# A two-layer hybrid backbone: gate and up of ten tiles in each of two feed-forwards by a seven-product scheme

## The chip, the cores and the metric

The kernel runs on one core of one Trainium2 chip, in one launch. Its time is the device time of that launch in microseconds (us). Before the change the median of three runs is 1741.17 us (1740.06 to 1743.56).

## The reference, cut to what matters

A sequence of 256 latent and 256 context tokens of width 1024 goes through two layers. Each layer is a half-step SwiGLU feed-forward (hidden width 2816), a token mixer with an output projection, and a second half-step feed-forward. Every one of the three is preceded by an RMS norm whose output is shifted and scaled by values that depend on the conditioning (adaLN), and followed by a gate from the same source. In the last layer only the latent tokens go through the mixer's queries, the output projection and the second feed-forward.

```
def _swiglu(u, w_gate, w_up, w_down):
    return (jax.nn.silu(u @ w_gate) * (u @ w_up)) @ w_down

mod_x = (jax.nn.silu(c) @ w_ada[l] + b_ada[l])[:, None, :]      # nine vectors of 1024: sh, sc, g three times
mod_c = jax.nn.silu(c_ctx) @ w_ada[l] + b_ada[l]                # the same for the context tokens
h  = h  + 0.5 * g1  * _swiglu(_modulate(_rms_norm(h,  norm_ffn1[l]), sh1,  sc1),  w_gate, w_up, w_down)
hc = hc + 0.5 * cg1 * _swiglu(_modulate(_rms_norm(hc, norm_ffn1[l]), csh1, csc1), w_gate, w_up, w_down)
```

## The kernel before, in words

**Data and precision.** Activations lie transposed: 128 partitions by 8 blocks of the width by 512 tokens (columns 0 to 255 latent, 256 to 511 context). Every float32 operand of a large product is kept as a high part that TensorE's fp32r format holds exactly and a low part that is the rest. One 128x128 block of weights against the tokens is then three matmuls in `mm3` (L133 to L136): high by high, high by low, low by high. `U` is the normed and modulated input of a stage, `U[0]` (`Uh`) its high part and `U[1]` (`Ul`) its low part.

**Weights.** `wload` (L126) loads 512 KB over SP's queue into one of three `raw` buffers, copies it on ScalarE to the high half of one of four `split` buffers (L129), and subtracts on VectorE to get the low half (L130). So each 512 KB of weights cost one ScalarE and one VectorE instruction of 128x1024 elements, and three matmuls per 128x128 block wait for them.

**Feed-forward.** `ffn` goes over 22 tiles of 128 hidden units, in parts of 6, 6, 6 and 4. `up_one` computes gate and up of one tile: 24 matmuls into the PSUM tile `pg`, 24 into `pu`. `evac` makes silu(gate) on ScalarE (L371), times up on VectorE (L372), and the high and low halves of `G` (L373, L374). After the first tile of a part the products with the down matrix of the part before it run (`down`, `pd`, L234 adds them to the residual `H`). The last part's down products run in halves of 256 columns together with the next norm. In the second layer's second feed-forward all matmuls have 256 columns. The stages are called here ffn1, mixer and ffn2 of layer 0 and 1.

**adaLN products.** Each of the 72 blocks of 128 modulation values per layer is a row-wise dot product on VectorE: `ada_dve` loads 512 KB over GpSimd's queue into `araw` and runs one scalar_tensor_tensor with accumulation per token (L151, output `ascr`, one instruction for the latent conditioning and one for the context's). `ada_jobs` makes a list of such jobs, and `run_jobs` issues them evenly over the tiles of a feed-forward; ffn1 of layer 0 has 48 blocks, ffn2 of layer 0 32, ffn1 of layer 1 48 (32 of them for the latent conditioning alone), ffn2 of layer 1 none. `cb` holds silu of the conditioning, loaded and computed once per stage.

**Order.** Each engine runs its queue strictly in order. A scheduler places the instructions of the program in the queues; the start of the program and the mixers follow written tables.

Of the kernel before, what the change touches and what calls it, by code (L numbers as in the profile page):

```python
# [18 lines left out]
TOK = SEQ + CTX  # L19
# [4 lines left out]
ABUFS = 8  # L24
# [36 lines left out]
def hybrid_backbone(ctx: ExitStack, tc: tile.TileContext, I, out):  # L61
# [83 lines left out]
    def ada_dve(l, ft, cb, ntok, pool):
        raw = pool.tile([128, 1024], F32, tag="araw", name="araw", bufs=ABUFS)
        with tc.issue_after(marks["pool"]):
            nc.gpsimd.dma_start(raw, I["w_adaT"][l, :, ft * 1024:(ft + 1) * 1024])
        scr = pool.tile([128, 1024], F32, tag="ascr", name="ascr", bufs=1)
        for t in range(ntok):  # L150
            stt(scr, raw, 1.0, cb[:, t, :], op0=ALU.mult, op1=ALU.mult, accum_out=ada[l][:, ft, t:t + 1])  # L151
# [109 lines left out]
    def first_tiles(pool, csel, U, src):  # L261
# [14 lines left out]
        def a(p, i):  # L276

            if i == 0:
                ada_ps[p] = bank("mm", "adaps")
            c, b = divmod(i, 2)  # L280
            raw = pool.tile([128, 4, 256], F32, tag="araw", name="araw", bufs=ABUFS)
# [20 lines left out]
        def w(i):  # L302
            raw = raw_load(src(i), 1024)
            if i < 4:
                t = wp.tile([128, 2, 1024], F32R, tag="split", name="split", bufs=4)
                parts = [(t, 0, 1024)]
            else:
                parts = [(pool.tile([128, 2, 512], F32R, tag="G", name="split0", bufs=10), o, 512) for o in (0, 512)]
            for t, o, n in parts:
                act(t[:, 0, :], raw[:, o:o + n], AF.Copy)  # L310
            sps.append((raw, parts))

        def x(i):
            raw, parts = sps[i]
            for t, o, n in parts:
                tt(t[:, 1, :], raw[:, o:o + n], t[:, 0, :].bitcast(F32), ALU.subtract)
# [19 lines left out]
        def m(i, f):  # L336
            t, o, _ = sps[i][1][f // 4 if i >= 4 else 0]
            wh, wl = (t[:, e, f * 128 - o:f * 128 - o + 128] for e in range(2))
# [11 lines left out]
    def ffn(l, w, halves, pool, U, jobs, after, start=None):  # L350
        both = len(halves) == 2
# [7 lines left out]
        def run_jobs(frac):  # L359
            nonlocal done  # L360
            while done < min(njobs, math.ceil(frac * njobs)):
# [3 lines left out]
        def chunk(src, ft):  # L365
            return wload(src[l, :, ft * 1024:(ft + 1) * 1024])

        def evac(pg, pu):
            g = pool.tile([128, 2, TOK], F32R, tag="G", name="G", bufs=10)
            sil = pool.tile([128, TOK], F32, tag="sil", name="sil", bufs=2)  # L370
            act(sil[:, cols], pg[:, cols], AF.Silu)  # L371
            tt(sil[:, cols], sil[:, cols], pu[:, cols], ALU.mult)  # L372
# [21 lines left out]

        G = {}
        off = [0]

        def down(p0, n, last):
            if not last:
                for d in range(KT):  # L400
                    sp = wload(wd[l, :, off[0]:off[0] + n * 128], n * 128)
                    off[0] += n * 128
                    ps = bank("mm", "pd")
                    for k in range(n):
                        mm3(ps[:, cols], sp[:, 0, k * 128:k * 128 + 128], sp[:, 1, k * 128:k * 128 + 128],
# [3 lines left out]
            else:  # L409
                sps = []  # L410
                for i in range(KT // 2):
                    sps.append(wload(wd[l, :, off[0]:off[0] + n * 256], n * 256))
                    off[0] += n * 256
                def piece(ps, d, h):
                    c = (LAT, CT)[h]
                    o = (d % 2) * n * 128
                    for k in range(n):
                        mm3(ps[:, :256], sps[d // 2][:, 0, o + k * 128:o + k * 128 + 128],
                            sps[d // 2][:, 1, o + k * 128:o + k * 128 + 128],
# [6 lines left out]
        for pi, n in enumerate(PARTS):  # L426
            j = 0
            while j < n:
# [6 lines left out]
                elif ft == 0 and both:  # L435
                    G[0], G[1] = up_two(0)
                    j += 2
                else:
                    G[ft] = up_one(ft)
                    j += 1  # L440
                run_jobs((p0 + j) / (FT - 3))
# [5 lines left out]
            else:  # L447
                run_jobs(1.0)
# [4 lines left out]
    def mixer(l, pool, U):  # L453
# [4 lines left out]
        perm, rope, maskA, maskC, hsel, qkg, sink, nsink, qg8 = (  # L458
            late[n] for n in ("perm", "rope", "maskA", "maskC", "hsel", "qkg", "sink", "nsink", "qg8"))

        def qk_chunk(i):
            return wload(win[l, :, i * 1024:(i + 1) * 1024])

        def rope_lat(x):
            sw = bank("mm", "sw")
            mm(sw[:, :256], perm, x[:, LAT], start=True, stop=True)
            a = pool.tile([128, 256], F32, tag="ra", name="ra", bufs=1)
            b = pool.tile([128, 256], F32, tag="rb_", name="rb_", bufs=1)
# [106 lines left out]
        def v_tok(sps, nk, n, dst, t):  # L575
            ps = bank("mm", "pv")
            for k in range(KT):
                s, o = sps[k // nk], (k % nk) * n
                c = slice(t * 128, t * 128 + 128)
                mm(ps[:, :n], U[0][:, k, c], s[:, 0, o:o + n], start=(k == 0), stop=False)  # L580
                mm(ps[:, :n], U[0][:, k, c], s[:, 1, o:o + n], start=False, stop=False)
                mm(ps[:, :n], U[1][:, k, c], s[:, 0, o:o + n], start=False, stop=(k == KT - 1))
# [188 lines left out]
    def out_proj(l, halves, Y, qcols, after):  # L771
# [5 lines left out]
        for part in range(2):  # L777
            sps = []
            if part == 0:
                for d in range(KT):  # L780
                    if d % 2 == 0:
                        i = d // 2
                        sp = wload(I["w_out"][l, :, i * 1024:(i + 1) * 1024])
# [4 lines left out]
            else:  # L788
                sps = [wload(I["w_out"][l, :, (4 + i) * 1024:(5 + i) * 1024]) for i in range(4)]
# [18 lines left out]
    def ada_jobs(l, mods, pool, ntok=2):  # L808
        jobs = []
        for m in mods:  # L810
            i = MODS.index(m)
            for d in range(KT):
                def job(ft=i * KT + d, m=m, fin=(d == KT - 1)):
                    ada_dve(l, ft, load_cb(pool), ntok, pool)
# [5 lines left out]
    for l in range(DEPTH):  # L820
        last = l == DEPTH - 1
        with tc.tile_pool(name=f"ffn1_{l}", bufs=1) as pool:
            start = None
            if l == 0:
                csel = pool.tile([128, KT, 4, 32], F32, name="csel")
# [18 lines left out]
            else:  # L844
                jobs = ada_jobs(1, ("shm", "scm"), pool) + ada_jobs(1, ("gm", "sh2", "sc2", "g2"), pool, 1)
# [9 lines left out]
        with tc.tile_pool(name=f"ffn2_{l}", bufs=1) as pool:  # L855
            if not last:
                jobs = ada_jobs(0, ("g2",), pool) + ada_jobs(1, ("sh1", "sc1", "g1"), pool)
            else:
                jobs = []
# [22 lines left out]
def _layout(x, c, ctx, c_ctx, w_ada, b_ada, norm_ffn1, w_ffn1_gate, w_ffn1_up, w_ffn1_down, norm_mix, w_in,  # L882
# [13 lines left out]
    for w, (wg, wu, wd) in (("1", (w_ffn1_gate, w_ffn1_up, w_ffn1_down)),  # L896
# [7 lines left out]
        a[f"w_ffn{w}_down"] = np.concatenate(parts, 2)  # L904
    qk = np.concatenate([w_in[:, :, :1024], w_in[:, :, 1024:1152], w_in[:, :, 1280:1408], w_in[:, :, 1536:1920]], 2)
# [43 lines left out]
```

## Time and profile before

| | us |
|---|---|
| median of three runs | 1741.17 |
| the profiled execution's own time | 1742.45 |
| its span in the trace | 1740.5 |
| TensorE busy | 1700.8 |
| VectorE busy | 1180.0 |
| ScalarE busy | 718.5 |
| GpSimd busy | 165.8 |

All durations below come from the one profiled execution. Matmuls overlap in the trace: one of 256 columns is shown with 0.28 us while the next starts 0.12 us later, so the cost of a matmul is the distance from one start to the next, or a window's length over its count. VectorE's instructions overlap a little in the same way. The stages in the trace: ffn1 of layer 0 about 22 to 398 us, the mixer and output projection to 627, ffn2 of layer 0 to 996, ffn1 of layer 1 to 1362, the mixer and output projection to 1529, ffn2 of layer 1 to 1730.

### The profile page before, as it was taken

Reading aid. Unit: us, or ns where it says so; the run is one execution under the profiler, and the core shown is the slowest. Engines: PE = TensorE matmul, PEld = TensorE weight load, DVE = VectorE, ACT = ScalarE, POOL = GpSimd, SP = SyncE. Lnnn points to the kernel's source line nnn. Section 1 sums busy time; section 2 is a strip of 40 time slices with the busy share of each in tenths; the row PEclk is TensorE's granted clock in tenths of the full one; section 3 lists DMA queues with packets and bytes.
Section 4 is the critical chain, followed back from the end, with each engine's and each line's share of the span. In section 5 each row is a group of like instructions: output and inputs, shape, how many; then the busy total and the mean of one; then the engine's idle time right before and its main releaser. Section 6 shows DMA issues by size and latency. Waiting matters only on the chain.

```text
span 1740.5 us, 24756 instructions
## 1 busy us (share of the span) xinstructions
PE 1700.8 (98%) x9572; PEld 1477.5 (85%) x9572; DVE 1180.0 (68%) x2031; ACT 718.5 (41%) x1206; POOL 165.8 (10%) x251
## 2 busy tenths in 40 slices
PE   7999999999999999999999999999999999989997
PEld 4888888889888898888888898888888888889997
DVE  5899963447978869983334599934343787965555
ACT  4322222235888653222222442222222577754443
POOL 0311100012102031100000212100000211100000
PEclk9999999999999999999999999999999999989999
DMA  8877643323223247743333288824332333356663
GB/s 330 309 240 243 197 117 84 110 73 115 58 82 85 75 169 238 236 129 89 108 85 109 63 319 277 321 79 115 85 109 86 99 84 102 109 155 182 182 176 113
DMA packets 76693, 258.37 MB, mean 148 GB/s; under 512 B 8944, under 2 KB 11248, under 8 KB 76192
## 3 DMA queue, kind: packets, MB, share of 16 engines
q1 hardware_dynamic: 54096, 176.72, 33.2%
q0 software_dynamic: 21760, 79.38, 14.3%
q8 instruction: 75, 1.23, 0.3%
q10 hardware_dynamic: 720, 0.69, 0.1%
q14 instruction: 42, 0.34, 0.1%
HBM read 250.47 MB, written 1.05 MB: 145 GB/s over the span
## 4 chain that ended last, share of the span: by engine, by line
PE 89%; DVE 4%; ACT 4%; issue 2%; POOL 1%; DMA 1%; POOLq 0%; DVEq 0%; SPq 0%; ACTq 0%
PE pd L135 8%; PE pd L134 8%; PE pd L136 8%; PE pu L134 8%; PE pu L135 8%; PE pu L136 8%; PE pg L134 8%; PE pg L136 8%; PE pg L135 8%; PE pq L136 1%; PE pq L134 1%; PE pq L135 1%; PE pt L679 1%; DVE split L130 1%; PE pv L580 1%
## 5 line engine op out<-in xcount | busy, mean ns | idle before, releaser
L129 ACT ACTIVATE split<-raw 128x1024 fp32r<-128x1024 f32 (+1 forms) x336 | 332.7, 991 | 546.6 <-PE pu L136 223.2
L130 DVE TENSOR_TENSOR split<-raw,split 128x1024 fp32r<-128x1024 f32 (+1 forms) x336 | 383.9, 1143 | 234.1 <-ACT split L129 233.2
L151 DVE SCALAR_TENSOR_TENSOR ascr<-araw,cb 128x1024 f32<-128x1024 f32 x224 | 273.3, 1220 | 9.9 <-ACT cb L804 7.0
L135 PE MATMUL pd<-G,split 128*128 128x512 f32 (+1 forms) x800 | 272.5, 341 | 0.0
L134 PE MATMUL pd<-G,split 128*128 128x512 f32 (+1 forms) x800 | 271.5, 341 | 0.0
L136 PE MATMUL pd<-G,split 128*128 128x512 f32 (+1 forms) x800 | 271.4, 340 | 0.0
L134 PE MATMUL pg<-Uh,split 128*128 128x512 f32 (+1 forms) x712 | 252.4, 355 | 2.1 <-ACT Uh L225 2.1
L136 PE MATMUL pg<-Uh,split 128*128 128x512 f32 (+1 forms) x712 | 252.3, 354 | 0.0
L135 PE MATMUL pg<-Ul,split 128*128 128x512 f32 (+1 forms) x712 | 252.0, 355 | 0.1
L134 PE MATMUL pu<-Uh,split 128*128 128x512 f32 (+1 forms) x712 | 252.1, 354 | 0.0
L135 PE MATMUL pu<-Ul,split 128*128 128x512 f32 (+1 forms) x712 | 251.9, 354 | 0.0
L136 PE MATMUL pu<-Uh,split 128*128 128x512 f32 (+1 forms) x712 | 251.9, 354 | 0.0
L234 DVE SCALAR_TENSOR_TENSOR H<-pd,ada,H 128x256 f32<-128x256 f32 x272 | 123.3, 479 | 106.9 <-PE pd L136 106.8
L135 PEld LDWEIGHTS pd<-G,split 128*128 128x128 f32 x800 | 151.6, 190 | 17.2
L136 PEld LDWEIGHTS pd<-G,split 128*128 128x128 f32 x800 | 151.4, 190 | 16.9
L134 PEld LDWEIGHTS pd<-G,split 128*128 128x128 f32 x800 | 151.1, 189 | 17.3
L134 PEld LDWEIGHTS pg<-Uh,split 128*128 128x128 f32 x712 | 135.4, 190 | 21.0 <-ACT Uh L225 2.6
L135 PEld LDWEIGHTS pg<-Ul,split 128*128 128x128 f32 x712 | 135.4, 190 | 18.6 <-DVE Ul L226 0.3
L136 PEld LDWEIGHTS pu<-Uh,split 128*128 128x128 f32 x712 | 135.2, 190 | 18.5
L136 PEld LDWEIGHTS pg<-Uh,split 128*128 128x128 f32 x712 | 135.2, 190 | 18.4
L134 PEld LDWEIGHTS pu<-Uh,split 128*128 128x128 f32 x712 | 135.3, 190 | 18.3
L135 PEld LDWEIGHTS pu<-Ul,split 128*128 128x128 f32 x712 | 135.0, 190 | 18.4
(199 smaller groups left out, 2412.6 us busy)
## 6 DMA issues: line engine op xcount, KB each, us to landing
araw<-in_w_adaT POOLq DMA_DIRECT2D x128, 512.0 KB, 5.0
raw<-in_w_ffn_gate SPq DMA_DIRECT2D x88, 512.0 KB, 3.8
raw<-in_w_ffn_up SPq DMA_DIRECT2D x88, 512.0 KB, 3.9
raw<-in_w_ffn_down SPq DMA_DIRECT2D x96, 384.0 KB, 3.2
raw<-in_w_in SPq DMA_DIRECT2D x26, 512.0 KB, 3.5
araw<-in_w_ada SPq DMA_DIRECT2D x16, 512.0 KB, 9.9
raw<-in_w_ffn_down SPq DMA_DIRECT2D x16, 512.0 KB, 3.6
raw<-in_w_out SPq DMA_DIRECT2D x16, 512.0 KB, 3.7
```

Source lines behind the costliest of these rows:

```text
L129: act(sp[:, 0, :n], raw[:, :n], AF.Copy)
L130: tt(sp[:, 1, :n], raw[:, :n], sp[:, 0, :n].bitcast(F32), ALU.subtract)
L134: mm(ps, wh, xh, start=first, stop=False)
L135: mm(ps, wh, xl, start=False, stop=False)
L136: mm(ps, wl, xh, start=False, stop=last)
L151: stt(scr, raw, 1.0, cb[:, t, :], op0=ALU.mult, op1=ALU.mult, accum_out=ada[l][:, ft, t:t + 1])
L234: stt(H[:, d, cols], ps[:, off:off + 256], gate[:, d, half:half + 1], H[:, d, cols], op0=ALU.mult, op1=ALU.add)
L580: mm(ps[:, :n], U[0][:, k, c], s[:, 0, o:o + n], start=(k == 0), stop=False)
L679: nc.tensor.transpose(pt[:, k * 128:(k + 1) * 128], P[t][:, k * 128:(k + 1) * 128], ident)
```

## The change

**Seven products instead of eight.** `FAST` names ffn2 of layer 0 and ffn1 of layer 1, from tile 12 on: ten tiles, taken as five pairs by `up_fast`. For a pair the tokens are cut in two halves (latent, context), the width 1024 in two halves of 512, and the 256 hidden units in two tiles, for gate and up each: a 2x2 by 2x2 block product, computed by seven block products instead of eight (Winograd's form of Strassen's scheme). Each product has 24 matmuls (gate and up, four blocks of 128, three matmuls each) of 256 columns, so a pair has 168 matmuls of 256 columns where it had 96 of 512.

**What the scheme needs besides.** `forms` (after tile 7) and `last_form` (in the first pair) make the sums and differences of `U`: 13 VectorE instructions and 4 ScalarE instructions of 128x1024 elements per feed-forward. Each pair takes four 512 KB blocks of weights (a new copy in DRAM in the order needed, `w_fast`) and makes three more from them with four VectorE subtractions; seven splits instead of four; and the products are put together with eight VectorE instructions of 512 elements and two of 256 (two of these make the low halves of `G`). `w0`, `w1`, `t2` and `cc` have one buffer each.

**Jobs moved.** In these two feed-forwards 65% of the adaLN jobs are issued up to tile 10 and the rest from the second pair on (`run_jobs` in `up_fast`), each product held behind the marked VectorE instruction (`marks["dve"]`). The gate `g2` of layer 1 moves from ffn1 to the first five tiles of ffn2 of layer 1, with its own `cb`. The 224 adaLN products stay 224. `araw` has three buffers in the two feed-forwards instead of eight, `G` eight instead of ten.

**A shifted low half.** The `split` buffer is 2176 elements wide, and wherever the matmuls have 256 columns (the products of the scheme, the last down products, the second half of the output projection, layer 1's queries and output projection, all of ffn2 of layer 1) the low half starts 8 elements, 32 bytes, later than it did.

**Small moves.** The mask `maskC` is loaded in each mixer instead of once, and the rotary temporaries share buffers with the norm's.

```diff
-def wload(src, n=1024):
-    raw = raw_load(src, n)
-    sp = wp.tile([128, 2, 1024], F32R, tag="split", name="split", bufs=4)
-    act(sp[:, 0, :n], raw[:, :n], AF.Copy)
-    tt(sp[:, 1, :n], raw[:, :n], sp[:, 0, :n].bitcast(F32), ALU.subtract)
-    return sp
+def halves_of(pad):
+    t = wp.tile([128, 2176], F32R, tag="split", name="split", bufs=4)
+    o = 1024 + (8 if pad else 0)
+    return t[:, :1024], t[:, o:o + 1024]
+
+def wload(src, n=1024, pad=False):
+    return split(raw_load(src, n), n, pad)
+
+def split(raw, n=1024, pad=False):
+    hi, lo = halves_of(pad)
+    act(hi[:, :n], raw[:, :n], AF.Copy)
+    tt(lo[:, :n], raw[:, :n], hi[:, :n].bitcast(F32), ALU.subtract)
+    return hi, lo
...
+            with tc.issue_after(marks["dve"]) if "dve" in marks else nullcontext():
+                stt(scr, raw, 1.0, cb[:, t, :], op0=ALU.mult, op1=ALU.mult, accum_out=ada[l][:, ft, t:t + 1])
...
+        def run_jobs(ft):
+            nonlocal done
+            if l and not both:
+                frac = ft / 5
+            elif fast == FT:
+                frac = ft / (FT - 3)
+            else:
+                late_ = max(0, ft - fast - 2) / (FT - fast - 4)
+                frac = EARLY * min(1, ft / (fast - 2)) + (1 - EARLY) * late_
...
+        def up_fast(ft):
+            i0 = (ft - fast) * 2
+            src = lambda i: I[f"w_fast{l}{w}"][:, (i0 + i) * 1024:(i0 + i + 1) * 1024]
+            b11, b12 = fm["w"]
+            nc.sync.dma_start(b11, src(0))
+            nc.sync.dma_start(b12, src(1))
+            b22 = raw_load(src(2), 1024)
+            b21 = raw_load(src(3), 1024)
+            t2 = pool.tile([128, 1024], F32, tag="t2", name="t2", bufs=1)
+            A, X, Y, Z = bank("s", "pa"), bank("t", "px"), bank("s", "py"), bank("t", "pz")
...
+            prod(A, b11, "11", True)
+            p1 = c22
+            act(p1, two(A), AF.Copy)
+            tt(b11, b12, b11, ALU.subtract)
+            tt(t2, b22, b11, ALU.subtract)
+            prod(X, t2, "S2", True)
+            marks["dve"] = ins_of(tt(u2, two(X), p1, ALU.add))
+            run_jobs(ft + 0.7)
+            prod(Y, b11, "S1", True)
+            tt(b12, b22, b12, ALU.subtract)
+            prod(Z, b12, "S3", True)
+            u3 = pool.tile([128, TOK], F32, tag="sil", name="u3", bufs=2)
+            tt(two(u3), two(Z), u2, ALU.add)
+            marks["dve"] = ins_of(tt(c22, two(Y), two(u3), ALU.add))
+            run_jobs(ft + 1.4)
+            if ft == fast:
+                last_form()
+            prod(A, b21, "12", False)
...
+            tt(t2, t2, b21, ALU.subtract)
+            X = bank("t", "px2")
+            prod(X, t2, "22", True)
+            tt(u3, u3, X, ALU.subtract)
...
+            prod(Y, b22, "S4", False)
+            tt(u2, two(Y), u2, ALU.add)
...
-                jobs = ada_jobs(1, ("shm", "scm"), pool) + ada_jobs(1, ("gm", "sh2", "sc2", "g2"), pool, 1)
+                jobs = ada_jobs(1, ("shm", "scm"), pool, 2, 3) + ada_jobs(1, ("gm", "sh2", "sc2"), pool, 1, 3)
...
-                jobs = []
+                jobs = ada_jobs(1, ("g2",), pool, 1)
```

**The order of VectorE's queue around tiles 15 and 16 of ffn2 of layer 0, before.** `split` is a low half of weights, `sil` and `G` belong to `evac`; what a row waits for stands in brackets.

```order
L130 TENSOR_TENSOR split_7517<-raw_7515,split_7517 128x1024 [waits DMAHW5_49,PE_49,Activation_49]
L372 TENSOR_TENSOR sil_7427<-sil_7427,pu_7367 128x512 [waits PE_49]
L130 TENSOR_TENSOR split_7546<-raw_7544,split_7546 128x1024 [waits DMAHW6_49,Activation_49]
L374 TENSOR_TENSOR G_7426<-sil_7427,G_7426 128x512 [waits Activation_49]
L130 TENSOR_TENSOR split_7593<-raw_7591,split_7593 128x1024 [waits DMAHW7_49,PE_49,Activation_49]
L372 TENSOR_TENSOR sil_7498<-sil_7498,pu_7438 128x512 [waits PE_49]
L130 TENSOR_TENSOR split_7622<-raw_7620,split_7622 128x1024 [waits DMAHW0_49,Activation_49]
L374 TENSOR_TENSOR G_7497<-sil_7498,G_7497 128x512 [waits Activation_49]
```

For each tile two splits and an evacuation of two instructions stand here, and no adaLN product.

**The same place after: VectorE's queue from the end of the pair 14, 15 to the split for the second product of the pair 16, 17.** `ascr` rows (L163) are adaLN products; `w0` and `t2` are the differences of weights of the next pair, `px`, `py`, `px2` PSUM tiles of products.

```order
L513 TENSOR_TENSOR u3_7530<-u3_7530,px2_7571 128x512 [waits PE_49]
L177 SCALAR_TENSOR_TENSOR amod1_88<-ada1_86,gains_79 128x16 [waits DVE_49]
L492 TENSOR_TENSOR w0_6655<-w1_6656,w0_6655 128x1024 [waits DMAHW5_49]
L515 TENSOR_TENSOR sil_7567<-sil_7567,u3_7530 128x256 [waits Activation_49]
L517 TENSOR_TENSOR cc_7406<-py_7404,cc_7406 128x2x256 [waits PE_49]
L493 TENSOR_TENSOR t2_7649<-raw_7645,w0_6655 128x1024 [waits DMAHW3_49,DVE_49]
L519 TENSOR_TENSOR cc_7406<-cc_7406 128x512 [waits Activation_49]
L524 TENSOR_TENSOR G_7632<-sil_7567,G_7632 128x512
L163 SCALAR_TENSOR_TENSOR ascr_7640,ada1_86<-araw_7638,cb_5954 128x1024 [waits DMASW1_49]
L524 TENSOR_TENSOR G_7635<-cc_7406,G_7635 128x512 [waits Activation_49]
L163 SCALAR_TENSOR_TENSOR ascr_7640,ada1_86<-araw_7638,cb_5954 128x1024 [waits DVE_49]
L140 TENSOR_TENSOR split_7685<-t2_7649,split_7685 128x1024
```

The low half that the second product of the pair 16, 17 needs (`split<-t2`, the last row) now stands behind the whole evacuation of the pair 14, 15 and behind two adaLN products.

**VectorE's queue at the start of ffn2 of layer 1, before.**

```order
L372 TENSOR_TENSOR sil_13269<-sil_13269,pu_13209 128x256 [waits DMASW3_49,DMASW4_49,DMASW2_49,DMASW5_49,DMASW1_49,DMASW6_49,DMASW0_49,DMASW7_49,PE_49,Activation_49]
L130 TENSOR_TENSOR split_13344<-raw_13342,split_13344 128x1024 [waits DMAHW2_49,Activation_49]
L374 TENSOR_TENSOR G_13268<-sil_13269,G_13268 128x256 [waits Activation_49]
L130 TENSOR_TENSOR split_13373<-raw_13371,split_13373 128x1024 [waits DMAHW3_49,Activation_49]
L372 TENSOR_TENSOR sil_13335<-sil_13335,pu_13275 128x256 [waits PE_49]
L130 TENSOR_TENSOR split_13410<-raw_13408,split_13410 128x1024 [waits DMAHW4_49,Activation_49]
L374 TENSOR_TENSOR G_13334<-sil_13335,G_13334 128x256 [waits Activation_49]
L130 TENSOR_TENSOR split_13439<-raw_13437,split_13439 128x1024 [waits DMAHW5_49,Activation_49]
```

The first split of the third tile stands right behind the first tile's `sil`.

**The same place after.**

```order
L394 TENSOR_TENSOR sil_14233<-sil_14233,pu_14173 128x256 [waits DMASW3_49,DMASW4_49,DMASW2_49,DMASW5_49,DMASW1_49,DMASW6_49,DMASW0_49,DMASW7_49,PE_49,Activation_49]
L163 SCALAR_TENSOR_TENSOR ascr_14243,ada1_86<-araw_14241,cb_14238 128x1024 [waits DMASW4_49]
L396 TENSOR_TENSOR G_14232<-sil_14233,G_14232 128x256 [waits Activation_49]
L163 SCALAR_TENSOR_TENSOR ascr_14247,ada1_86<-araw_14245,cb_14238 128x1024 [waits DMASW5_49,DVE_49]
L394 TENSOR_TENSOR sil_14310<-sil_14310,pu_14250 128x256 [waits PE_49]
L163 SCALAR_TENSOR_TENSOR ascr_14317,ada1_86<-araw_14315,cb_14238 128x1024 [waits DMASW6_49,DVE_49]
L396 TENSOR_TENSOR G_14309<-sil_14310,G_14309 128x256 [waits Activation_49]
L163 SCALAR_TENSOR_TENSOR ascr_14321,ada1_86<-araw_14319,cb_14238 128x1024 [waits DMASW7_49,DVE_49]
L140 TENSOR_TENSOR split_14327<-raw_14325,split_14327 128x1024 [waits DMAHW2_49]
L140 TENSOR_TENSOR split_14356<-raw_14354,split_14356 128x1024 [waits DMAHW3_49]
L140 TENSOR_TENSOR split_14397<-raw_14395,split_14397 128x1024 [waits DMAHW4_49]
```

Four adaLN products (L163) and the second tile's `sil` and `G` now stand ahead of that split.

## Rows read from the trace of the kernel before

**Rows 1.** The page: busy time by engine, TensorE's granted clock in 40 slices, the chain by engine
```profile
PE 1700.8 (98%) x9572; PEld 1477.5 (85%) x9572; DVE 1180.0 (68%) x2031; ACT 718.5 (41%) x1206; POOL 165.8 (10%) x251
...
PEclk9999999999999999999999999999999999989999
...
PE 89%; DVE 4%; ACT 4%; issue 2%; POOL 1%; DMA 1%; POOLq 0%; DVEq 0%; SPq 0%; ACTq 0%
```

**Rows 2.** Windows: busy us (count) of PE, PEld, DVE, ACT, POOL, clock, DMA, GB/s, DMA share, GB/s
```profile
200.00:300.00 100.00, 100.00 (x442) 82.80 (x442) 59.15 (x90) 26.29 (x33) 1.07 (x2) 1.00 0.39 113
839.50:904.00 64.50, 64.50 (x286) 53.43 (x285) 21.22 (x24) 17.59 (x23) 0.00 (x0) 1.00 0.32 90
1600.00:1700.00 100.00, 100.00 (x836) 100.00 (x835) 58.23 (x78) 44.83 (x63) 0.00 (x0) 1.00 0.63 183
1526.00:1543.00 17.00, 12.37 (x71) 11.73 (x70) 12.73 (x25) 7.80 (x17) 2.86 (x3) 0.70 0.41 124
```

**Rows 3.** Groups of VectorE by line and shape: count | busy us, mean ns | idle before
```profile
L130 DVE TENSOR_TENSOR split<-raw,split 128x1024 fp32r<-128x1024 f32 x232 | 284.7, 1227 | 171.6 <-ACT split L129 171.5
L151 DVE SCALAR_TENSOR_TENSOR ascr<-araw,cb 128x1024 f32<-128x1024 f32 x224 | 273.3, 1220 | 9.9 <-ACT cb L804 7.0
L372 DVE TENSOR_TENSOR sil<-sil,pu 128x256 f32<-128x256 f32 x22 | 9.3, 421 | 11.6 <-PE pu L136 11.6
```

**Rows 4.** Timeline of VectorE in ffn1 of layer 0: start, duration, instruction, [idle before]
```profile
102.08 1.22 DVE L151 SCALAR_TENSOR_TENSOR ascr<-araw,cb 128x1024 f32<-128x1024 f32 x1
103.23 0.69 DVE L374 TENSOR_TENSOR G<-sil,G 128x512 fp32r<-128x512 f32 x1
103.83 1.22 DVE L151 SCALAR_TENSOR_TENSOR ascr<-araw,cb 128x1024 f32<-128x1024 f32 x1
104.97 0.95 DVE L130 TENSOR_TENSOR split<-raw,split 128x768 fp32r<-128x768 f32 x1
```

**Rows 5.** Timeline of VectorE around one feed-forward tile, ffn2 of layer 0
```profile
883.21 0.69 DVE L372 TENSOR_TENSOR sil<-sil,pu 128x512 f32<-128x512 f32 x1 [2.58 <-PE pu L136]
884.31 1.23 DVE L130 TENSOR_TENSOR split<-raw,split 128x1024 fp32r<-128x1024 f32 x1 [0.40 <-ACT split L129]
885.45 0.68 DVE L374 TENSOR_TENSOR G<-sil,G 128x512 fp32r<-128x512 f32 x1
```

**Rows 6.** Timeline of VectorE, the first tiles of ffn2 of layer 1
```profile
1547.06 0.42 DVE L372 TENSOR_TENSOR sil<-sil,pu 128x256 f32<-128x256 f32 x1 [3.97 <-PE pu L136]
1547.89 1.23 DVE L130 TENSOR_TENSOR split<-raw,split 128x1024 fp32r<-128x1024 f32 x1 [0.41 <-ACT split L129]
1549.03 0.42 DVE L374 TENSOR_TENSOR G<-sil,G 128x256 fp32r<-128x256 f32 x1
1549.69 1.23 DVE L130 TENSOR_TENSOR split<-raw,split 128x1024 fp32r<-128x1024 f32 x1 [0.24 <-ACT split L129]
1551.09 0.42 DVE L372 TENSOR_TENSOR sil<-sil,pu 128x256 f32<-128x256 f32 x1 [0.17 <-PE pu L136]
1551.42 1.22 DVE L130 TENSOR_TENSOR split<-raw,split 128x1024 fp32r<-128x1024 f32 x1
```

**Rows 7.** Timeline of TensorE between the output projection and ffn2, layer 1
```profile
1531.46 0.35 PE L201 MATMUL ss<-ones,acc 128*128 128x2 f32 x2 [2.22 <-DVE acc L193]
1536.67 0.58 PE L134 MATMUL pg<-Uh,split 128*128 128x256 f32 x1 [1.11 <-ACT Uh L225]
1537.05 0.41 PE L134 MATMUL pu<-Uh,split 128*128 128x256 f32 x1
1537.26 0.41 PE L134 MATMUL pg<-Uh,split 128*128 128x256 f32 x1
```

**Rows 8.** Timeline of VectorE, the last tile of ffn2 of layer 0
```profile
970.25 0.69 DVE L372 TENSOR_TENSOR sil<-sil,pu 128x512 f32<-128x512 f32 x1 [2.58 <-PE pu L136]
972.49 0.68 DVE L374 TENSOR_TENSOR G<-sil,G 128x512 fp32r<-128x512 f32 x1
```

**Rows 9.** The page: DMA issues by group, KB each, median us to landing
```profile
araw<-in_w_adaT POOLq DMA_DIRECT2D x128, 512.0 KB, 5.0
```

More of the change, by code (lines that the diff above doesn't have):

```diff
@@ L1 @@
 import math
-from contextlib import ExitStack
+from contextlib import ExitStack, nullcontext
 import numpy as np
@@ L350, in ffn @@
     def ffn(l, w, halves, pool, U, jobs, after, start=None):
+        fast = FAST.get((l, w), FT)
+        gbufs = 8 if fast < FT else 10
         both = len(halves) == 2
@@ L393, in up_two, with forms, whole, parts @@
             return [evac(pss[0], pss[1]), evac(pss[2], pss[3])]
+        fm = {}
+        def forms():
+            LO, HI = slice(0, 4), slice(4, 8)
+            rows = lambda t: t.rearrange("p (a b) -> p a b", a=4)
+            block = [pool.tile([128, 1024], F32R, name=f"S{i}", bufs=1) for i in range(6)]
+            w1, w2 = fm["w"] = [pool.tile([128, 1024], F32, name=f"w{i}", bufs=1) for i in range(2)]
+            w3 = pool.tile([128, 1024], F32, tag="t2", name="w3", bufs=1)
+            def whole(t, k, c):
+                with tc.issue_after(marks["dve"]):
+                    tt(rows(t), U[0][:, k, c].bitcast(F32), U[1][:, k, c].bitcast(F32), ALU.add)
+            def parts(n, i, t):
+                h, lo = block[2 * i:2 * i + 2]
+                act(h, t, AF.Copy)
+                tt(lo, t, h.bitcast(F32), ALU.subtract)
+                fm[n] = (rows(h), rows(lo))
+            whole(w1, LO, CT)
+            whole(w2, HI, CT)
+            tt(w2, w1, w2, ALU.add)
+            parts("S1", 0, w2)
+            whole(w3, LO, LAT)
+            tt(w1, w3, w1, ALU.subtract)
+            parts("S3", 1, w1)
+            tt(w3, w2, w3, ALU.subtract)
+            parts("S2", 2, w3)
+            for n, k, c in (("11", LO, LAT), ("12", HI, LAT), ("22", HI, CT)):
+                fm[n] = (U[0][:, k, c], U[1][:, k, c])
@@ new lines, in last_form @@
+        def last_form():
+            h, lo = fm["S4"] = U[0][:, 0:4, CT], U[1][:, 0:4, CT]
+            rows = lambda t: t.rearrange("p (a b) -> p a b", a=4)
+            a, b = (rows(pool.tile([128, 1024], F32, tag="araw", name="s4", bufs=3)) for _ in range(2))
+            tt(a, U[0][:, 4:8, LAT].bitcast(F32), U[1][:, 4:8, LAT].bitcast(F32), ALU.add)
+            tt(b, fm["S2"][0].bitcast(F32), fm["S2"][1].bitcast(F32), ALU.add)
+            tt(a, a, b, ALU.subtract)
+            act(h, a, AF.Copy)
+            tt(lo, a, h.bitcast(F32), ALU.subtract)
@@ L400, in down @@
                 for d in range(KT):
-                    sp = wload(wd[l, :, off[0]:off[0] + n * 128], n * 128)
+                    sp = wload(wd[l, :, off[0]:off[0] + n * 128], n * 128, not both)
                     off[0] += n * 128
@@ L440, in ffn @@
                     j += 1
-                run_jobs((p0 + j) / (FT - 3))
+                run_jobs(p0 + j)
+                if fast < FT and p0 + j == fast - LEAD:
+                    forms()
                 if pend is not None:
@@ L457, in mixer @@
         win = I["w_in"]
-        perm, rope, maskA, maskC, hsel, qkg, sink, nsink, qg8 = (
-            late[n] for n in ("perm", "rope", "maskA", "maskC", "hsel", "qkg", "sink", "nsink", "qg8"))
+        perm, rope, maskA, hsel, qkg, sink, nsink, qg8 = (
+            late[n] for n in ("perm", "rope", "maskA", "hsel", "qkg", "sink", "nsink", "qg8"))
+        maskC = pool.tile([128, 2, 256], F32, name="maskC", bufs=1)
+        nc.gpsimd.dma_start(maskC, I["maskC"])
         def qk_chunk(i):
-            return wload(win[l, :, i * 1024:(i + 1) * 1024])
+            return wload(win[l, :, i * 1024:(i + 1) * 1024], pad=i < 8 and not ctxq)
         def rope_lat(x):
@@ L788, in out_proj @@
             else:
-                sps = [wload(I["w_out"][l, :, (4 + i) * 1024:(5 + i) * 1024]) for i in range(4)]
+                sps = [wload(I["w_out"][l, :, (4 + i) * 1024:(5 + i) * 1024], pad=True) for i in range(4)]
                 def piece(ps, d, h):
```

105 lines of the change are left out of this document (69 added, 36 removed).

## The prediction

> **What bounds the kernel now.** I read the page's busy times and its chain first: TensorE is busy for 98% of the span, it makes 89% of the chain that ended last, and no other engine has more than 4% of it [rows 1]. Then the windows, one per kind of stage, because an average over the span hides what each stage lacks: in a dense stretch of 512 columns TensorE never rests while VectorE has 59.15 us of work in 100; in the tiles 13 to 18 of ffn2 of layer 0, just where the change goes, VectorE works only 21.22 us of 64.5 [rows 2]. So time is TensorE's matmuls, and what is taken from them is time as long as VectorE, which makes every low half, stays ahead. The timelines then give the price of one instruction and the slack that a tile leaves.
>
> **Prices.** A matmul of 512 columns: 100 us / 442 = 0.2262 us; the middle window gives 64.5 / 286 = 0.2255, and a few records can be missing, so 0.2266. One of 256 columns: 100 / 836 = 0.1196, taken as 0.120 [rows 2]. So half the columns cost 53%, not half. On VectorE I take the distance from start to start: 1.14 us for 1024 elements (1547.89 to 1549.03) and 0.33 for 256 (1551.09 to 1551.42) [rows 6], 0.60 for 512 and 1.145 for an adaLN product (102.08 to 103.23 to 103.83 to 104.97) [rows 4]; the means of 1.227 and 1.220 us [rows 3] overlap the next instruction.
>
> **Gain on TensorE.** Per feed-forward ten tiles x 48 = 480 matmuls x 0.2266 = 108.8 us become five pairs x 168 = 840 x 0.120 = 100.8: 8.0 us less, 16.0 for both. One eighth fewer products gives only 7% because of the dearer columns. By column count alone the gain would be 13.6 each.
>
> **Load on VectorE.** A pair has eleven instructions of 1024 (seven splits, four differences), eight of 512 and two of 256: 12.54 + 4.80 + 0.66 = 18.0 us, against 168 x 0.120 = 20.2 us of TensorE. Before, two tiles took four splits and four of 512, 4.56 + 2.40 = 7.0 us, beside 21.8. So 11% of room is left in a pair, and into it the change puts adaLN products: by the order of VectorE's queue 22 in the pairs 14, 16 and 18 of ffn2 of layer 0, 25.2 us, and 14 in those of ffn1 of layer 1. Between these three pairs no down products stand, so TensorE needs 60.5 us and VectorE 54.0 + 25.2 = 79.2 in the first.
>
> How much of this comes through as waiting I take from the order, in us from the first product of pair 14. VectorE's combination of the second product can start at 2 x 2.88 = 5.76. From there to the low half for pair 18's second product stand 18 of 1024, 16 of 512, 4 of 256, 16 adaLN products: 20.5 + 9.6 + 1.3 + 18.3 = 49.7, with 0.2 of small ones 49.9. So that half is ready at 55.7. TensorE would ask for it at 2 x 20.16 + 2.88 = 43.2. After it come six products, 17.3, less 0.7 that may be issued ahead (the high-half matmuls): the stretch ends at 72.3 to 72.7 instead of 60.5, 12.2 lost. In ffn1 of layer 1 the same stretch has 18 of 1024, 15 of 512, 4 of 256 and 9 adaLN products: 41.3, ready at 47 to 48, end 64.2: 3.7 lost. Here the evacuation rows of before matter: sil and G stood at 883.21 and 885.45 with 2.58 us of idle time ahead [rows 5], and nothing waited; in the new order the evacuation and two adaLN products stand ahead of the split that the next product needs.
>
> **What is hidden.** The forms of U, 13 x 1.14 = 14.8 us of VectorE in each feed-forward, lie under tiles 8 to 11 (43.5 us of TensorE) and pair 12; the tightest split there has about 0.6 us to spare, so I take 0, and up to +2 if that goes. The products that leave these late tiles for early ones go to stretches with 40 idle us in 100 [rows 2]: 0. ScalarE gets seven copies in place of four, under 20.2 us: 0. SP issues the four blocks of a pair; the loads of w0 and w1 wait for their single buffers but are issued a product or more ahead of use: 0. GpSimd's loads take 5.0 us to land [rows 9]; three buffers in place of eight hold the loads back for as long as VectorE is late, and a group of four products needs about what three buffers hold: 0, up to +2. The mask and rotary buffers: 0, up to +1 in each mixer.
>
> **Tails.** The last pair ends with two evacuations in place of one: its last low half of G comes 24.6 us after the pair's start, 4.4 after its last product, where before G started 2.24 us after sil [rows 8]. The last down products are cut in pieces that need G in turn; I take 0.9 us per feed-forward, 1.8 in all, 0 to 4.
>
> **Start of ffn2 of layer 1.** In before the split of the third tile starts at 1547.89, in the shade of the second tile's matmuls, and the second tile's sil at 1551.09 [rows 6]. In the new queue that sil and four adaLN products stand ahead of the split: after 1551.09, 0.33 + 1.145 + 0.33 + 1.145 and a ScalarE hand-over put it near 1555.2. TensorE wants it at 1551.1, or 0.7 later as above: +3.4. The cb of this stage lands under the norm; if it came late, up to +3 more.
>
> **Clock.** Where TensorE rested 2.22 us, then worked on small matmuls between waits, the granted clock fell: the window has 0.70 [rows 2], and matmuls of 256 columns then stand 0.213 apart (1537.05 to 1537.26) [rows 7]: the level of 1.2 GHz. The stall of ffn2 of layer 0 falls into lumps, one of about 4 us at the start of pair 16, others of 3 to 5 us later. One stretch at the lower level that costs 1.7 us is my value, since rows show such a stretch only after idle time beside sparse work; 0 to 12 are the bounds. The Trainium skill has the rule (page "TensorE: Matmul & The Clock Gate", section "HAM oscillation — how this bites in real kernels") that idle gaps between bursts throttle TensorE again; rows 7 agree for the norm, no row shows it inside a feed-forward. By it every lump would cost, which is a rival below.
>
> **The shifted low half.** No row of before has such a layout, so it is bounded. 0.213 at half the clock is 256 columns at 1.2 GHz with no gap; at full clock that would be 0.1067, and the measured 0.120 has 0.0133 of something on top. Outside the pairs 2736 matmuls of 256 columns get the shift (by the code's loops 1584 in ffn2 of layer 1, 576 last down products of the other stages, 384 of the output projections, 192 queries). If it took all of the gap: -36 us; if only from the third of them that loads the low half: -12; and in the two pairs per feed-forward that TensorE bounds, 672 matmuls, -9 or -3 more. It could cost as well: up to +10. I take 0, since the one pitch of 0.120 stands in ffn2 of layer 1 with weights, and equally where activations are the weights. The Trainium skill (page "TensorE: Matmul & The Clock Gate", section "Step-by-step: what each phase is for") says that TensorE reads weights and moving data by two independent ports, so a load takes nothing from the running matmul; by that rule the shift is worth 0; the trace can't tell.
>
> **Sum.** -16.0 + 12.2 + 3.7 + 1.8 + 3.4 + 1.7 = +6.8 on the profiled execution's 1742.45, so 1749.3. That execution is 1.3 above the median of the runs, so 1748 for a median.
>
> **Rivals.**
> 1. The shift makes 256 columns cheaper. For it: 0.0133 us of every matmul is not streaming, and it is gone at half the clock. Against it: no row varies with the layout. With a third of it, 1748 - 12 - 3 = 1733; with all, 1748 - 36 - 9 = 1703. It decides the sign from about 0.002 us per matmul on (7 us / 3408): below that it is still slower. This is the case on the other side.
> 2. VectorE keeps up: the products and splits of one pair slide under the next, or the real distances are shorter in a dense queue. For it: the stretch before has two thirds of VectorE free. Against it: 79.2 us do not go into 60.5. Without the 15.9 of stalls and the clock's 1.7, 1748 - 17.6 = 1730. It needs VectorE's distances at about three quarters of the rows.
> 3. The stalls throttle TensorE. Four or five lumps in the first feed-forward and one or two in the second, each followed by a stretch at 1.2 GHz that costs 1.7 to 3 us, less what VectorE catches up meanwhile: 1748 + 8 to 14, about 1758. For it the window at 0.70; against it that a slow TensorE gives VectorE the time it lacked.
>
> **How the numbers follow.** Forecast 0.42 (own range 1741 to 1755), rival 1 0.30, rival 2 0.17, rival 3 0.11. What this measurement can tell is 0.2%, 3.5 us: under 1737.7 faster, over 1744.7 slower. The forecast gives 0.31 slower, 0.10 the same, 0.01 faster; rival 1 0.26 faster, 0.03 the same, 0.01 slower; rival 2 0.16 faster, 0.01 the same; rival 3 0.11 slower. Together faster 0.43, same 0.14, slower 0.43. The range 1716 to 1757 leaves out the large gain of rival 1, about 0.08, and the far half of rival 3 with the unlikely sums of bounds, about 0.09.
>
> **What would show it.** The windows of pairs 14 to 18: TensorE idle with the releaser VectorE `split`, about 12 us in ffn2 of layer 0 and 4 in ffn1 of layer 1, VectorE at 95% or more there. Dense stretches of ffn2 of layer 1 with 0.120 per matmul, else rival 1. An idle row of 3 us at about the third tile of ffn2 of layer 1. The granted clock at 1.00 in pairs 14 to 18 but for one dip, else rival 3. The prediction is wrong if the dense 256-column distance changes, or if TensorE's idle time in the pairs is under 5 us.

## The result: 0.8% slower, and the profile after

The changed kernel takes 1755.57 us (median, 1753.34 to 1757.34) against 1741.81 of before: a ratio of 1.0078, 95% interval 1.0061 to 1.0096. The profiled execution took 1754.82 us. The page of the changed kernel, next to [rows 1]:

```profile
PE 1690.9 (96%) x10292; PEld 1500.0 (86%) x10292; DVE 1319.8 (75%) x2187; ACT 767.0 (44%) x1265; POOL 167.1 (10%) x253
...
PE 78%; DVE 11%; ACT 5%; issue 4%; DMA 2%; POOL 1%; POOLq 0%; DVEq 0%; SPq 0%; ACTq 0%
```

TensorE is busy 9.9 us less, and yet the end comes 12.5 us later: VectorE has 11% of the chain where it had 4%. Where it waits is seen in windows of the changed kernel, the pairs 14, 16 and 18 of ffn2 of layer 0 and a stretch of ffn2 of layer 1 (columns as in [rows 2]).

```profile
849.73:869.61 19.88, 19.88 (x169) 19.87 (x168) 17.32 (x27) 6.59 (x8) 1.59 (x3) 1.00 0.57 169
869.61:896.12 26.51, 22.86 (x170) 22.12 (x169) 24.90 (x36) 10.68 (x14) 1.58 (x3) 0.87 0.43 132
896.12:926.49 30.37, 24.67 (x170) 23.97 (x169) 28.73 (x38) 11.84 (x16) 1.05 (x2) 0.83 0.45 132
1600.00:1700.00 100.00, 100.00 (x848) 100.00 (x847) 59.41 (x79) 45.07 (x63) 0.00 (x0) 1.00 0.64 186
```

A pair without waiting takes 19.88 us; these three took 76.76 in place of 59.64: 17.1 us lost. VectorE is at 94 and 95% in the second and third. TensorE is idle for 3.65 + 5.70 us by its busy time, and the granted clock is 0.87 and 0.83, so part of each window runs at 1.2 GHz. The same three pairs of ffn1 of layer 1, where fewer products stand, and what follows them:

```profile
1225.50:1245.38 19.88, 19.88 (x169) 19.88 (x168) 16.87 (x24) 6.78 (x9) 2.11 (x4) 1.00 0.71 210
1245.38:1268.07 22.69, 21.63 (x170) 20.31 (x169) 22.56 (x30) 9.60 (x13) 2.11 (x4) 1.00 0.57 183
1268.07:1293.32 25.25, 23.41 (x175) 22.40 (x173) 22.88 (x33) 10.98 (x15) 1.59 (x3) 0.93 0.43 136
1293.32:1325.06 31.74, 31.74 (x142) 26.29 (x141) 23.28 (x35) 9.35 (x11) 0.00 (x0) 1.00 0.37 112
```

The third window also holds four of the 144 matmuls of the down products: the other 140 take the 31.74 us of the fourth, and all 144 take 32.67 us without waiting (a window of e5_downs below), so 0.93 us. Without these, 66.89 us in place of 59.64: 7.2 lost. The waits by name, TensorE's timeline in the changed kernel (the idle time before a row and its releaser stand in brackets):

```profile
877.38 0.58 PE L147 MATMUL px<-S,split 128*128 128x256 f32 x1 [2.01 <-DVE split L140]
...
899.29 0.58 PE L147 MATMUL pa<-Uh,split 128*128 128x256 f32 x1 [2.77 <-DVE split L140]
...
906.27 0.58 PE L145 MATMUL px<-S,split 128*128 128x256 f32 x1 [2.78 <-ACT split L139]
...
1564.77 0.58 PE L147 MATMUL pg<-Uh,split 128*128 128x256 f32 x1 [3.30 <-DVE split L140]
```

The third is named after ScalarE, which copies a high half that VectorE had first to make as a difference. The fourth stands at the third tile of ffn2 of layer 1. VectorE's timeline ahead of the first of them:

```profile
871.99 0.70 DVE L519 TENSOR_TENSOR cc<-cc 128x512 f32<-128x512 f32 x1
872.60 0.70 DVE L524 TENSOR_TENSOR G<-sil,G 128x512 fp32r<-128x512 f32 x1
873.20 1.23 DVE L163 SCALAR_TENSOR_TENSOR ascr<-araw,cb 128x1024 f32<-128x1024 f32 x1
...
874.94 1.23 DVE L163 SCALAR_TENSOR_TENSOR ascr<-araw,cb 128x1024 f32<-128x1024 f32 x1
...
876.09 1.24 DVE L140 TENSOR_TENSOR split<-t,split 128x1024 fp32r<-128x1024 f32 x1
```

No idle time stands between these rows: the split that TensorE asks for comes last, in the order that the change shows.

### The profile page after: what moved, and what is told of

Its sections match the earlier page's. It is cut to its first block, busy times and chain, and to the rows that moved or that the text cites. A ratio compares the mean times of both kernels' runs of the same rounds, so it can differ in the third digit from the quotient of the medians.

```text
span 1753.0 us, 26434 instructions
## 1 busy us (share of the span) xinstructions
PE 1690.9 (96%) x10292; PEld 1500.0 (86%) x10292; DVE 1319.8 (75%) x2187; ACT 767.0 (44%) x1265; POOL 167.1 (10%) x253
## 4 chain that ended last, share of the span: by engine, by line
PE 78%; DVE 11%; ACT 5%; issue 4%; DMA 2%; POOL 1%; POOLq 0%; DVEq 0%; SPq 0%; ACTq 0%
PE pd L147 8%; PE pd L146 8%; PE pd L145 8%; PE pg L147 5%; PE pg L145 5%; PE pu L147 5%; PE pu L145 5%; PE pg L146 5%; PE pu L146 5%; DVE ascr L163 3%; DVE split L140 3%; PE pq L147 1%; PE pq L145 1%; PE pq L146 1%; PE pt L820 1%
## 5 line engine op out<-in xcount | busy, mean ns | idle before, releaser
L140 DVE TENSOR_TENSOR split<-raw,split 128x1024 fp32r<-128x1024 f32 (+1 forms) x316 | 358.8, 1138 | 138.5 <-ACT split L139 137.3
L163 DVE SCALAR_TENSOR_TENSOR ascr<-araw,cb 128x1024 f32<-128x1024 f32 x224 | 273.6, 1221 | 2.3 <-DMA araw<-in_w_adaT 0.8
L147 PE MATMUL pg<-Uh,split 128*128 128x512 f32 (+1 forms) x552 | 190.5, 345 | 3.3 <-DVE split L140 3.3
L145 PE MATMUL pg<-Uh,split 128*128 128x512 f32 (+1 forms) x552 | 190.5, 346 | 2.5 <-ACT Uh L237 2.1
L146 PE MATMUL pg<-Ul,split 128*128 128x512 f32 (+1 forms) x552 | 189.5, 344 | 0.1
L145 PE MATMUL pu<-Uh,split 128*128 128x512 f32 (+1 forms) x552 | 189.5, 343 | 0.0
L147 PE MATMUL pu<-Uh,split 128*128 128x512 f32 (+1 forms) x552 | 189.4, 343 | 0.0
L146 PE MATMUL pu<-Ul,split 128*128 128x512 f32 (+1 forms) x552 | 189.0, 342 | 0.0
L159 POOL DMA_DIRECT2D araw<-in_w_adaT x128 | 68.0, 532 | 706.7 <-DVE ascr L163 653.6
L147 PEld LDWEIGHTS pg<-Uh,split 128*128 128x128 f32 x552 | 105.1, 190 | 15.7 <-DVE split L140 3.5
L145 PEld LDWEIGHTS pg<-Uh,split 128*128 128x128 f32 x552 | 105.2, 191 | 15.4 <-ACT Uh L237 2.6
L146 PEld LDWEIGHTS pg<-Ul,split 128*128 128x128 f32 x552 | 105.2, 191 | 12.3 <-DVE Ul L238 0.3
L145 PEld LDWEIGHTS pu<-Uh,split 128*128 128x128 f32 x552 | 104.4, 189 | 12.2
L146 PEld LDWEIGHTS pu<-Ul,split 128*128 128x128 f32 x552 | 104.4, 189 | 12.1
```

The costliest lines, as they stand in the source:

```text
L140: tt(lo[:, :n], raw[:, :n], hi[:, :n].bitcast(F32), ALU.subtract)
L145: mm(ps, wh, xh, start=first, stop=False, skip_group_check=go_on)
L146: mm(ps, wh, xl, start=False, stop=False, skip_group_check=go_on)
L147: mm(ps, wl, xh, start=False, stop=last, skip_group_check=go_on)
```

## The experiments

**Where the products stand: all early.** One number changed:

```diff
-LEAD, EARLY = 4, 0.65
+LEAD, EARLY = 4, 1.0
```

> All adaLN jobs of the two feed-forwards are issued up to tile 10, none in the pairs 14 to 20; everything else as changed. Theory (adaLN products fill VectorE's queue in the pairs 14 to 18, TensorE waits 11.9 us and runs 5.0 us of lower clock in ffn2 of layer 0, about 4 to 5 together in ffn1 of layer 1): the three pairs take 59.6 to 61 us instead of 76.8 and 64.3, so 1755.6 - 16 - 4 = 1735 to 1738, granted clock 1.00 in the pairs. Rival A (the single buffers w0, w1, t2 and cc chain one pair to the next, whatever VectorE else does): the idle rows in the pairs stay, 1752 to 1756. Rival B (the products only move the wait: tiles 0 to 11 now stall on VectorE): pairs free, but as much idle time in tiles 8 to 12, 1748 or more.

Measured 1754.26 us (ratio to before 1.0070, 1.0058 to 1.0082): hardly better, and yet the three pairs take 19.88 us each. The time went to the early tiles, rival B. A window of this run in ffn2 of layer 0, where the forms of U are made:

```profile
760.00:780.00 20.00, 15.55 (x70) 12.56 (x68) 20.00 (x28) 6.68 (x8) 1.59 (x3) 0.95 0.40 131
```

VectorE is full there, and TensorE's next row comes after 4.45 us of waiting for a split. In ffn1 of layer 1 idle rows of 4.18 and 2.07 us stand ahead of the pairs, where the changed kernel has none. The products had only met another crowded stretch; this run alone could not tell overload from a rule that products cost anywhere.

**The same products in the down stretches.**

```diff
-            run_jobs(ft + 0.7)
...
-            run_jobs(ft + 1.4)
...
+                    if fast < FT and p0 >= 6:      # in down, after each d
+                        run_jobs(FT, ((p0 // 6 - 1) * KT + d + 1) / (2 * KT))
```

> The late 35% of the adaLN jobs are issued in the down products of the second and third part (one step after each of 16 groups) instead of in the pairs; the early 65% stay. By the order 12 and 10 products of ffn2 of layer 0 and 7 and 7 of ffn1 of layer 1 stand there, none between the pairs 14 and 18. Theory (a stretch stalls when VectorE's work in that stretch exceeds TensorE's; with all jobs early it was the tiles up to 9 that overflowed): the downs have 32.4 us of TensorE and 13.3 of VectorE each, so they take the products free, the pairs take 59.6 to 61 us, and 16.9 + 5 us go: 1755.6 - 22, 1732 to 1737. Rival A (the pairs wait on their single buffers and their chain): idle rows stay in the pairs, 1750 or more. Rival B (any place for the products costs the same, since a held-back product always meets a split): idle rows in the downs, 1748 or more.

Measured 1730.68 us (0.9932, 0.9920 to 0.9945): 24.9 us less than the change. The theory had 22; the 17.1 and 7.2 us lost in the pairs are 24.3. Windows of this run, the three pairs and the down products behind them:

```profile
850.09:869.97 19.88, 19.88 (x169) 19.88 (x168) 16.45 (x19) 8.49 (x10) 0.00 (x0) 1.00 0.36 106
869.97:889.85 19.88, 19.88 (x170) 19.88 (x169) 18.48 (x22) 10.39 (x13) 0.00 (x0) 1.00 0.34 100
889.85:909.73 19.88, 19.88 (x170) 19.88 (x169) 15.83 (x20) 10.18 (x14) 0.00 (x0) 1.00 0.47 134
909.73:942.40 32.67, 32.67 (x147) 27.04 (x145) 32.17 (x52) 8.89 (x11) 1.05 (x2) 1.00 0.39 117
```

The scheme, its buffers and its chain are the same; without adaLN products in these pairs TensorE never waits and the clock stays. The down stretch takes them to 32.17 us of 32.67, without a loss. So the scheme is worth its gain, and the change lost it by the place of 36 instructions.

**g2 two tiles later.** `frac = max(0, ft - 2) / 5` in place of `ft / 5`.

> The eight g2 jobs of ffn2 of layer 1 are issued from tile 3 to tile 7 instead of 1 to 5. Theory (four products and two evacuation steps ahead of the third tile's split cost 3.3 us of idle time and 1.1 us of lower clock): no idle row over 1 us at the third tile, 1755.6 - 4.4 = 1751. Rival (the stage waits for its cb, its loads or ScalarE, wherever the products stand): an idle row of 3 us stays, perhaps later, 1755.

Measured 1748.72 us (1.0047, 1.0033 to 1.0061): 6.9 less, more than the 4.4 expected; the idle row of 3.30 us is gone, and none over 1.1 stands in its place. In the profiled executions ffn2 of layer 1 takes 194.9 us in place of 200.6, 5.7 less. One of the six runs took 1755.03 us, so the size beyond 4.4 lies within what the two medians leave open.

**The shift.** In e2_noshift `o = 1024` for all; e7_shiftonly is the kernel before with the shift alone (but for the rotary temporaries' buffers and the wider `split` tile, which stay as changed in all runs on the kernel before); e8_shiftall has `o = 1024 + 8` for every split; e9_shift64 has 16 elements in place of 8.

> The changed kernel with every low half of weights at its old place, 4096 bytes behind the high half; the order of all queues is the same. Theory (the shift is worth 0.0018 us of every matmul of 256 columns, 0.1182 against 0.1200): in 1600 to 1700 us 836 matmuls again instead of 848; 2736 x 0.0018 = 4.9 us outside the pairs and 1 to 3 in them, so 1761 to 1763. Rival (the denser count comes from something else in this kernel, or is given back as waiting for VectorE): 1755.6 and 846 to 848 matmuls in the window.

> The kernel before, with the low halves shifted by 32 bytes wherever the matmuls have 256 columns, and nothing else; the order of every queue is that of before. Theory (0.0018 us of each of 2736 matmuls): 1742.3 - 4.9, 1736 to 1739, 846 to 848 matmuls in 1600 to 1700 us. Rival (the shift pays only in the changed kernel's queues): 1742.

> As e7_shiftonly, but every low half is shifted, those for 512 columns too. Theory I (the shift helps each load of a low half, whatever streams meanwhile): 512 columns fall from 0.2266 by 0.0018, so about 10 us less than e7_shiftonly, 1727. Theory II (it helps only where a weight load and 256 columns take about the same time): 442 matmuls in 200 to 300 us as before, the time of e7_shiftonly within 2 us.

> As e7_shiftonly, with a shift of 64 bytes in place of 32. Theory I (any shift off the 4096 bytes between high and low half does it): 846 to 848 matmuls in 1600 to 1700 us and the time of e7_shiftonly, 1739.6 within 2. Theory II (the 32 bytes matter, the place within a 64-byte line): 836 matmuls and the time of before, 1742.7 within 2.

Without it the change takes 1759.24 us (1.0099 of before, 1.0086 to 1.0112), 3.7 more, less than was expected, and the window from 1600 to 1700 us has 835 matmuls where it had 848. In ffn2 of layer 0 the two kernels take the same time from norm to norm (377.0 and 377.1 us): there, what the shift gives in the pairs goes into waiting. With the shift alone the kernel before takes 1739.63 (0.9983, 0.9974 to 0.9992), with 64 bytes 1739.09 (0.9980, 0.9971 to 0.9989). Shifted everywhere it takes 1768.74 (1.0149, 1.0136 to 1.0163): neither theory had a loss. Windows of ffn2 of layer 1 with 32 bytes (e7_shiftonly):

```profile
1600.00:1700.00 100.00, 100.00 (x847) 100.00 (x846) 59.94 (x80) 44.62 (x63) 0.00 (x0) 1.00 0.65 188
```

with 64 bytes (e9_shift64):

```profile
1600.00:1700.00 100.00, 100.00 (x852) 100.00 (x851) 59.55 (x79) 45.71 (x64) 0.00 (x0) 1.00 0.64 187
```

and 512 columns with a shift of 32 bytes (e8_shiftall), in ffn1 of layer 0:

```profile
200.00:300.00 100.00, 100.00 (x430) 80.39 (x429) 60.59 (x93) 25.66 (x32) 1.61 (x3) 1.00 0.39 112
```

Against 836 and 442 [rows 2]: 256 columns gain 1.3 or 1.9%, 512 columns lose 2.8%.

**Everything but the scheme.** `FAST = {}`.

> The seven-product scheme is not used anywhere; everything else of the change stays: shifted low halves, products held behind the marked instruction, three araw buffers, g2 in ffn2 of layer 1. Theory (outside the pairs the change is -4.9 us of shift, +4.4 at the third tile of ffn2 of layer 1, about +1 elsewhere): 1741.8 + 0.5, so 1741 to 1743. Rival (the job order, the three buffers or the held-back products cost by themselves): 1747 or more.

Measured 1749.09 us (1.0038, 1.0026 to 1.0050): the rival. With `FAST` empty the jobs are also spread over the tiles as before and `G` has ten buffers again, so this run doesn't test the 65% order. e5_downs, with the scheme, takes 18.4 us less than this run. Of the 6.8 us over before, -3.1 are the shift and +6.9 g2 by the runs above, so 3.0 were to be found, or 4.2 with the 5.7 of the profiled executions. Two runs on the kernel before looked for them: the mask loaded in each mixer (e10_mask), and the products held behind the marked instruction (e11_hold).

> The kernel before, with the mask of the neighbourhood heads loaded on GpSimd's queue at the start of each mixer instead of once. Theory (GpSimd's two additions of the mask start 0.7 to 2.2 us later and then run beside VectorE's low halves of U, whose two instructions take 2.95 us in place of 0.87 to 1.91): about 1.0 us in each mixer, 1742.7 + 2.0 = 1744 to 1746. Rival (the longer VectorE instructions have slack behind them): 1742 to 1743.5.

> The kernel before, with each adaLN product held back behind the marked evacuation instruction in VectorE's queue, nothing else. Theory (holding back bunches the products of the first feed-forward between down products: an idle row of 0.9 to 1.2 us at about 126 us, and little elsewhere): 1743.5 to 1745. Rival (the idle row there comes from the buffers): 1742 to 1743.

The mask: 1744.57 us (1.0014, 1.0005 to 1.0023), +1.9 as expected. TensorE's wait for the next split of weights grows from 0.53 to 1.77 us in the first mixer and from 0.26 to 1.56 in the second. VectorE and GpSimd at the start of the first mixer of e10_mask:

```profile
402.62 2.97 DVE L238 SCALAR_TENSOR_TENSOR Ul<-t,ada,Uh 128x256 fp32r<-128x256 f32 x2
...
402.57 2.73 POOL L742 TENSOR_TENSOR bias<-bias,maskC 128x512 f32<-128x512 f32 x2 [2.69 <-DMA bias<-in_rpb]
```

Holding back: 1742.38 us (0.9998, 0.9990 to 1.0007), nothing; that theory falls. The idle row of 0.90 us at 126 us in the changed kernel, which neither e10_mask nor e11_hold has, and 1 to 2 us with it, stay unexplained; the three `araw` buffers were not run by themselves.

**The parts together.** e6_all is e5_downs with g2 later, the mask on SP's queue and the products held back only where the scheme is; e12_best has the 64-byte shift besides.

> As e5_downs, with the g2 jobs of ffn2 of layer 1 from tile 3 on, the mask loaded over SP's queue and the products held back only in the two feed-forwards with the scheme. Theory: the single gains add up: 1734 - 6.9 of g2 - about 1 of the first feed-forward - 0 to 2 of the mixers: 1724 to 1728, and faster than before. Rival (the gains share one cause, such as the clock's level, and do not add): 1730 to 1735.

> e6_all with the 64-byte shift of e9_shift64. Theory (852 matmuls in 100 us of ffn2 of layer 1 instead of 847 with 32 bytes, 0.0007 us of each of 4416 matmuls of 256 columns): 1723.1 - 3, 1719 to 1722. Rival (no difference between the two shifts, as the times of e7_shiftonly and e9_shift64 lie within each other's spread): 1722 to 1724.

Measured 1723.07 us (0.9894, 0.9879 to 0.9909) and 1721.26 (0.9887, 0.9870 to 0.9903): both faster than before and after. The gains add: the 7.6 us from e5_downs to e6_all are close to g2's 5.7 to 6.9 and the mask's 1.9. The second shift's 1.8 us are not separated from the spread of the two runs.

## Why the prediction was right

The sign and its cause were right: VectorE could not do its pairs and the products in TensorE's time. The size was not: the profiled executions differ by +12.4 us, predicted +6.8. The prediction gave slower and faster the same chance, 0.43, and the measured 1755.57 lies above the forecast's own range (1741 to 1755) and near the end of the whole one (1757). That the sign and the range held is in part luck. By its steps:

| step | predicted | measured |
|---|---|---|
| matmuls of the ten pairs | -16.0 | -18.8: ten times 19.88 against two tiles, 96 x 0.2266 = 21.76; about 3 of it the shift |
| waiting and clock, ffn2 of layer 0 | +12.2 +1.7 | +17.1 |
| waiting, ffn1 of layer 1 | +3.7 | +7.2 with its clock |
| tails | +1.8 | +1.9: idle rows of 0.73, 0.11 and 0.11 in each feed-forward |
| third tile of ffn2 of layer 1 | +3.4 | 3.30 idle in the trace; +5.7 to +6.9 by e3_g2later |
| mask in the mixers | 0 | +1.9 |
| shift outside the pairs | 0 | -3.1 |

The measured steps add up to +11.9 to +13.1. Most of what the sum missed is in the clock, in ffn1 of layer 1 and behind the third tile; the shift and the cheaper pairs took some of it back.

The first mis-sized term is the clock: "one stretch at the lower level that costs 1.7 us". The stretches of the changed kernel in which the granted clock is 0.50, three in ffn2 of layer 0 and one in ffn1 of layer 1:

```profile
875.00:881.82 6.82, 4.81 (x23) 4.50 (x23) 5.73 (x7) 2.60 (x3) 0.53 (x1) 0.50 0.52 140
898.89:902.30 3.41, 3.01 (x14) 3.01 (x15) 3.41 (x6) 0.63 (x1) 0.00 (x0) 0.50 0.36 132
905.72:912.54 6.82, 6.12 (x27) 5.83 (x28) 6.29 (x6) 3.34 (x4) 0.00 (x0) 0.50 0.49 155
1274.37:1277.77 3.40, 3.40 (x19) 3.40 (x18) 2.33 (x4) 0.60 (x1) 0.53 (x1) 0.50 0.62 171
```

TensorE is busy for 13.94 us in the first three and 3.40 in the fourth. Matmuls of 256 columns stand 0.213 us apart there, as in [rows 7], and 0.1183 (19.88 / 168) in the pairs without waiting, so 0.445 of that time is lost: as an estimate 6.2 and 1.5 us. With the idle time, 9.35 and 2.90 us, that is 15.6 of the 17.1 and 4.4 of the 7.2 lost; the rest is in breaks that show as little or no idle time, since a matmul is shown with 0.28 us while the next can start after 0.118. The prediction's own sign, a clock of 1.00 "but for one dip, else rival 3", thus spoke for rival 3: its mechanism was there, with four stretches in place of its five to seven, and 7.7 us of clock in the pairs, 6.0 above the forecast's term, where it had +8 to 14 on the whole. That a slower TensorE gave VectorE time in return is not measured; behind the first and the third of these stretches VectorE waited 1.61 and 0.72 us for TensorE's product.

The rule that the prediction cited from the Trainium skill (page "TensorE: Matmul & The Clock Gate", section "HAM oscillation — how this bites in real kernels"), that gaps between bursts throttle the engine, agrees here in kind inside a feed-forward: the clock fell around idle rows of 2.01, 2.77 and 2.78 us, and in ffn1 of layer 1 behind rows of 0.44 and 1.08 us. These are shorter than the waits of the page's own kernel. In e5_downs, without the waits, the clock of the pairs is 1.00.

The second is the waiting in ffn1 of layer 1. The prediction followed the queue to one split, that of pair 18's second product; the trace has idle rows at several products of pairs 16 and 18, from 0.10 to 1.08 us, some of them named after ScalarE's copy.

The third is the shift, taken as 0. The prediction named a changed 256-column distance as a sign that it was wrong, and the distance did change: rival 1's mechanism exists, at 0.0015 us of a matmul (100 / 836 less 100 / 847), below the 0.002 from which it was to decide the sign. The prediction put the shift at 0 by a sentence of the Trainium skill on two independent read ports (page "TensorE: Matmul & The Clock Gate", section "Step-by-step: what each phase is for"). That sentence does not cover what was measured, 847 and 430 matmuls against 836 and 442, and the measurement decides; no run shows what in TensorE depends on the address.

Rival 2, that VectorE keeps up, is refused by the idle rows; e5_downs shows what it takes: 18.0 us of work in a pair do fit under 19.88, the products on top do not. The cost named as hidden, 0 for the forms and the early products, held for 65% and fell for 100%, as e1_early shows. The mask was bounded with up to +1 in each mixer and came out there. The third tile's 3.30 us of idle time was foreseen to 0.1 us; behind it 14 matmuls ran at the lower level, which the sum left out.

## What to carry to other kernels

A trade of matmuls for additions is decided on the engine that adds: sum that engine's work stretch by stretch, in the order of its queue, against the time TensorE will then have. Background work on that engine belongs where its room is largest, here the down products between the pairs, which took ten of them and ended on time, and not spread by tile count. A stretch takes only what fits: with all products early, tiles and down products stalled in their turn. A wait of TensorE can cost more than its length: the time at the lower clock behind it belongs to the sum.

## What the runs showed of the hardware

- Where the low half of the weights starts changes the distance between matmuls, in both senses: with a start 32 or 64 bytes later 847 or 852 in place of 836 matmuls of 256 columns in 100 us, and with 32 bytes 430 in place of 442 of 512 columns. Whether the distance to the high half or the address itself does it was not separated.
- GpSimd's additions hold VectorE's up: two low halves of U take 0.87 us where no addition runs, and took 2.97 beside them in the first mixer of e10_mask (1.91 in the kernel before, where the additions had started 2.3 us ahead of them). The Trainium skill (page "SBUF — State Buffer", section "Who interferes with whom") has an exclusive port pair for which these two compete; the rows agree.
